# A new table of order for a two-layer hybrid encoder: where each part of a layer stands among the others, and how much a late choice of engine may bend it

## The chip, the cores and the metric

The kernel runs on one core of one Trainium2 chip, and the metric is device microseconds of one execution, measured from outside the program. The engines are named as the profile names them: PE is TensorE's matmul, PEld its weight load, DVE is VectorE, ACT is ScalarE, POOL is GpSimd, SP is SyncE, which issues the transfers. PEclk is the granted clock of TensorE as a share of 2.4 GHz; 0.50 is its lower level of 1.2 GHz. PSUM is the memory into which PE adds up its products, SBUF the one in which tiles lie.

## The reference

Two requests, a prompt of 256 tokens and a sample of 512, go through the same two layers; the kernel treats them as one block of 768 tokens with 1024 channels.

```
Layer:  h = RMSNorm(x) @ W_in, columns in four head groups
        [Fourier | differential attention | 2-D neighbourhood attention | bidirectional Mamba-2 SSD]
        x = x + concat(group outputs) @ W_out
        x = x + (silu(h2 @ w_gate) * (h2 @ w_up)) @ w_down,  h2 = RMSNorm(x)
Final RMSNorm.   D_MODEL = 1024, DEPTH = 2, D_FF = 2816, all in float32
```

The second half of a layer, SwiGLU, is called the FFN below; the first half, with its four head groups, the mixers.

## The kernel before

Float32 products are made of three matmuls in a faster format: each operand is split into a high part (a rounded copy) and a low part (operand minus high part), and low by high, high by high and high by low are added up in PSUM. Names ending in h and l are these parts. A split is therefore a copy (ACT or DVE) and a subtraction (DVE or POOL) for each tile.

**The FFN's gate and up products.** The 2816 columns are 22 blocks of 128, taken two by two as eleven pairs, `sp0` to `sp10`. The tokens are two halves of 384. With two column blocks, two halves of the input channels and two halves of the tokens, each of the matrices gate and up is a 2 by 2 block product, which is done with seven products of sums in place of eight (Strassen's way). A product is 12 matmuls of 128 by 128 by 384. `sums` makes the factors of the weights: it loads two tiles `raw` of 512 KB, splits the blocks a11 and a12, and then the sums s2, s3, s1, the block a22 and the sum s4, each into one tile `f` (its high and low part). `blocks0` and `blocks1` make the factors of the activations: b11 and b21 from token half 0 (norm `fnorm0`), and then t2, t3, t1, t4 and b22, sums over both token halves, once half 1 has its norm (`fnorm1`); `hb0` and `hb1` are the names of these parts. `first` is the products of b11 and b21, `rest` the other five, in the order t2, t3, t1, t4, b22. The results are combined on DVE (tiles u, v, c), go through Silu on ACT, and `hidden` multiplies gate by up and splits the result into ah and al.

Three pairs (`se0` to `se2`) run their `first` alone, 48 matmuls each, before `blocks1`, so that PE has work while half 1 gets its norm; their `rest` is then `sp0` to `sp2`, of 120 matmuls each. The other eight pairs have 168 each. Raw tiles of the weights have two places in SBUF (`NRAW`), so the next side's transfer can only start when the last reader of the one before is done.

**The down product** has three groups: `dn0` takes the pairs 8 to 10, whose ah and al stay in SBUF; `dn1` the pairs 0 to 3 and `dn2` the pairs 4 to 7, whose ah and al are written to DRAM (`ad`) and read back.

**What sets the order.** No engine's order is written by hand. `Schedule` takes down every operation with what it depends on, and `run` lays all of them out once, while the program is built. Each part of a layer (`self.at("sp3")` begins one) has two numbers in the table `SPAN`; an operation's key lies between them by its place in the part. Operations are sorted by key, and each engine in turn takes the first one that could start within `WAIT` of the moment at which the engine comes free. Where an operation has several ways (a copy on ACT or DVE, a subtraction on DVE or POOL), the way that ends first by the planner's costs is taken, `BIAS` being added to each engine's side:

```python
for (a, n, t), (b, *_) in zip(self.marks, self.marks[1:] + [(len(ops),)]):
    u, v = SPAN[n]
    for j in range(a, b):
        ops[j].key = t + u + (v - u) * ((j - a) / (b - a))
```

The planner also books a lock: an operation of DVE that reads two SBUF tiles, and any of POOL, is planned not to overlap the other's (`held`, `port`, `lock`). On the chip nothing of this plan's times is left, only each engine's order and the waits between engines.

Most instructions stand at lines of helpers: L402 is a matmul, L416 a transpose, L431 an activation, L435 a copy on ACT and L436 on DVE, L447 an operation with two tensors on DVE and L450 on POOL, L460 one with a scalar as well, L464 a reciprocal, L472 a reduction, L483 a transfer. In the changed kernel each is 8 lines further down.

Of the kernel before, what the change touches and what calls it, by code (L numbers as in the profile page):

```python
# [32 lines left out]
WCOLS = 1056  # L33
NSLOT, NRAW, NW, NE = 42, 2, 10, 11

WAIT = dict(PE=4, ACT=59, DVE=3, Pool=6017, Q=10)
BIAS = dict(ACT=0, DVE=300, Pool=100)
SWITCH = 255
OG = ((2, 3, 0, 1, 6, 7), (4, 5))
WPACK = 2  # L40
# [7 lines left out]
              dq0=256, dq1=384, dk0=512, dk1=640,  # L48
              nq0=1024, nq1=1152, nk0=1280, nk1=1408)
# [2 lines left out]
TABLES = {AF.Exp: 1, AF.Silu: 2, AF.Sqrt: 3}  # L52

SPAN = dict(
    fnorm0=(-8740.8, -65.3), dfin1=(-7110.3, -6348.1), dfin0=(-5181.3, -3413.1), nfin0=(-2877.4, -2819.9),
    nfin1=(-2414.8, -1862.3), fnorm1=(-1765.5, -951.1), dstk00=(-1305.8, -1205.9), dstk01=(-1140.4, -1140.4),
    sst3=(-1049.4, -990), sst5=(-947.2, -936.6), sst1=(-867, -703.1), sst6=(-864.1, -853.9), sst2=(-840.7, -648.3),
    sst4=(-740.6, -739.9), sst7=(-503.1, -498.1), sst0=(-460.4, -410.6), conv0=(-179.2, -128.4), sfin=(-99, 6.6),
    conv3=(-30.2, 11.6), fo1=(-28.8, 109.2), sch1=(-24.9, -9.3), da002=(-6, 19.9), dk1=(-5.9, -5.9),
    gate=(0.6, 16.8), norm=(2.5, 3.7), sscan=(6.4, 13.9), conv2=(17.2, 43.1), da001=(20.5, 110.7),  # L60
    da102=(20.8, 36.2), conv5=(21.2, 47.1), conv4=(42.3, 68.6), str4=(53.2, 111.3), conv1=(57.1, 57.1),
    sprep=(60.1, 72.6), dav=(66.8, 66.8), sch3=(91.5, 180.3), da100=(108.6, 115.8), sch0=(111.2, 146),
    str2=(111.6, 111.6), str0=(115.1, 134.8), str3=(123.7, 124.7), str1=(124, 124), str5=(134.7, 134.7),
    na01=(137.5, 166.3), dk0=(141.1, 183), sch5=(145.2, 148), dq0=(149.4, 149.4), sch4=(154.4, 155.1),
    sch2=(156.7, 185.3), ol=(164, 229), da012=(165.4, 215.3), fu=(175.8, 188.6), na00=(176.4, 191.1),
    da000=(183.3, 188.5), dq1=(185.2, 206.1), da004=(189.5, 201.5), fo0=(189.7, 203.4), ft=(192.8, 209.6),
    da010=(195.3, 216.1), da115=(195.6, 237.8), da005=(198.9, 200.8), da003=(202.5, 203.9), da011=(204.2, 222.9),
    fw=(208.6, 213.5), nk1=(209.2, 247.5), nav=(219.2, 245.6), da013=(220, 222), dstk10=(220.6, 220.6),
    da114=(221.9, 222.2), da105=(222.8, 231.8), da015=(223.9, 260), da103=(228.3, 228.5), da104=(229.1, 243.3),
    dstk11=(230.3, 230.3), da101=(234.6, 253.8), da014=(241.3, 248.8), nq0=(243.6, 256), da110=(245.2, 265.9),  # L70
    da113=(245.3, 246.2), na04=(246, 283.1), da112=(253.4, 253.4), nb0=(253.7, 281.3), da111=(257.5, 259.2),
    nk0=(262.3, 268), oa3=(265.2, 432.4), nq1=(269.8, 269.8), na05=(270.8, 314.2), na02=(271.6, 285),
    na03=(287.9, 327.5), na11=(291.1, 316.1), na12=(313.4, 322.2), nb1=(314.7, 349), oa4=(315.2, 342.8),
    na10=(320.3, 362.1), oa0=(328.4, 336.5), oa1=(335.9, 346.4), ow=(347.4, 373.5), oa6=(347.8, 355.8),
    na14=(369.5, 369.5), na15=(377.6, 405.7), na13=(377.9, 377.9), oa2=(385.6, 393.8), oa5=(409.1, 419.3),
    oa7=(425.8, 464.6), ob0=(449.7, 457.6), ob1=(458.4, 466.3),
    hb0=(457.5, 466), se0=(466.5, 467), se1=(467, 467.05), se2=(467.05, 467.1), hb1=(467.1, 468), xf=(467, 467.1),
    **{f"sp{p}": (470 + 28 * p, 498 + 28 * p) for p in range(11)},
    dn0=(778, 830), dn1=(830, 900), dn2=(900, 962), last=(938, 1006.8))

LAG = {("ACT", "ACT"): 153, ("DVE", "DVE"): 127, ("Pool", "Pool"): 102, ("ACT", "DVE"): 142, ("DVE", "ACT"): 140,
       ("ACT", "PE"): 281, ("DVE", "PE"): 244, ("ACT", "Pool"): 170, ("PE", "ACT"): 197, ("PE", "DVE"): 196,
# [9 lines left out]
class Schedule:  # L92
# [85 lines left out]
    def run(self):  # L178
# [32 lines left out]
        def port(o, e):  # L211
            return held["DVE" if e == "Pool" else "Pool"] if e in o.lock else 0.0
# [7 lines left out]
        def choose(e):  # L220
            f, pick = free[e], None
            for i, o in ready[e]:
# [13 lines left out]
                if len(o.ways) > 1:  # L236
                    c = next(w[1] for w in o.ways if w[0] == e) + BIAS.get(e, 0)
                    if any(max(free[w[0]], o.at[w[0]], port(o, w[0]), m) + w[1] + BIAS.get(w[0], 0) < s + c
                           for w in o.ways if w[0] != e):
                        continue  # L240
                if s <= f + WAIT[e] and (not o.table or o.table == table):
                    return s, i, o
# [1325 lines left out]
```

## Time and profile before

| | |
|---|---|
| three executions | 1857.09, 1849.77, 1855.98 us; median 1855.98 |
| profiled execution | 1856.15 us, of which the span from the first to the last instruction is 1854.4 |
| mean granted clock of TensorE | 0.986 |
| PE busy | 1771.5 us, 96% of the span |
| DVE, ACT, POOL busy | 1383.3, 794.2, 241.5 us |
| chain that ended last | PE 74%, DVE 16%, DMA 4%, ACT 3% |

The first row is the measure; the second is the one execution from which all rows of the trace come. A busy share is a mean over stages that have different limits, so the places at which PE stands idle matter, and what it waits for there.

### The profile page before, as it was taken

To read this page: it belongs to the slowest core of one execution; us is meant where nothing else is said; L and a number is where in the kernel's file an instruction comes from. 1 tells how busy PE (TensorE), PEld (TensorE's weight loads), DVE (VectorE), ACT (ScalarE), POOL (GpSimd) and SP (SyncE) were. 2 spreads that over 40 slices of the span, in tenths; PEclk is the share of its full clock that TensorE was granted. 3 is DMA by queue.
4 is the path that set the end of the run, shared out by engine and by line. 5 is a ranking of instruction groups with operands and counts; after the bars stand their busy time and mean duration, and the time that the engine had idled before them with its cause. 6 is when DMAs were issued, how large, how long until landed. Compare 5 with 4: busy or idle time off the path is not lost.

```text
span 1854.4 us, 28444 instructions
## 1 busy us (share of the span) xinstructions
PE 1771.5 (96%) x10600; PEld 1707.6 (92%) x10600; DVE 1383.3 (75%) x2646; ACT 794.2 (43%) x1660; POOL 241.5 (13%) x211
## 2 busy tenths in 40 slices
PE   8999899998899999999999988999889999999997
PEld 7998788997899999999999987889789999999987
DVE  7988897688778786434559989966978888764345
ACT  6454677463344443100234456755634344420013
POOL 0011020021131110000001211200212332110000
PEclk9999899999999999999999999999999999999999
DMA  6215446453444333642432154465343344265223
GB/s 211 91 35 157 145 145 224 146 185 103 142 136 137 113 114 119 235 162 66 113 113 74 38 162 156 136 228 176 113 142 137 116 146 137 80 229 187 92 89 114
DMA packets 96267, 252.45 MB, mean 136 GB/s; under 512 B 11648, under 2 KB 26368, under 8 KB 96128
## 3 DMA queue, kind: packets, MB, share of 16 engines
q1 hardware_dynamic: 96128, 250.62, 40.9%
q8 instruction: 84, 1.38, 0.3%
q14 instruction: 55, 0.45, 0.1%
HBM read 193.95 MB, written 56.62 MB: 135 GB/s over the span
## 4 chain that ended last, share of the span: by engine, by line
PE 74%; DVE 16%; DMA 4%; ACT 3%; issue 2%; SPq 0%; DVEq 0%; ACTq 0%
PE fm L402 34%; PE fs L402 27%; PE tok L402 6%; DMA raw<-w_up 2%; DVE f L447 1%; DVE up L447 1%; DVE nm L472 1%; DVE al L447 1%; PE ns L402 1%; DVE ex L460 1%; DVE s L447 1%; PE nv L402 1%; DMA stk<-qk 1%; DMA raw<-w_gate 1%; PE tr L416 1%
## 5 line engine op out<-in xcount | busy, mean ns | idle before, releaser
L402 PE MATMUL fm<-ah,w 128*128 128x384 f32 (+2 forms) x1408 | 268.2, 337 | 0.0
L402 PEld LDWEIGHTS fm<-ah,w 128*128 128x128 f32 x1408 | 242.9, 188 | 5.5
L402 PE MATMUL fm<-hh,w 128*128 128x384 f32 x896 | 196.0, 343 | 0.0
L447 DVE TENSOR_TENSOR w<-raw,w 128x1024 fp32r<-128x1024 f32 (+3 forms) x123 | 142.5, 1163 | 68.0 <-PE fm L402 40.3
L435 ACT ACTIVATE f<-s 128x512 fp32r<-128x512 f32 x174 | 108.4, 630 | 147.3 <-PE fs L402 81.5
L402 PEld LDWEIGHTS fm<-hh,w 128*128 128x128 f32 x896 | 158.4, 189 | 2.3
L447 DVE TENSOR_TENSOR X<-X,fm 128x384 f32<-128x384 f32 (+2 forms) x152 | 83.0, 550 | 93.8 <-PE fm L402 92.8
L402 PE MATMUL fm<-al,w 128*128 128x384 f32 (+2 forms) x704 | 142.9, 337 | 0.0
L402 PEld LDWEIGHTS fm<-al,w 128*128 128x128 f32 x704 | 123.0, 188 | 2.9
L447 DVE TENSOR_TENSOR f<-s,f 128x512 fp32r<-128x512 f32 x153 | 112.0, 739 | 16.0 <-ACT f L435 12.0
L402 PE MATMUL fm<-hl,w 128*128 128x384 f32 x448 | 113.4, 351 | 9.9 <-DVE hl L460 9.3
L402 PE MATMUL tok<-w,hh 128*128 128x256 f32 (+1 forms) x768 | 113.5, 285 | 0.0
L402 PE MATMUL fm<-oh,w 128*128 128x384 f32 x512 | 106.0, 341 | 0.0
L435 ACT ACTIVATE w<-raw 128x1024 fp32r<-128x1024 f32 (+3 forms) x70 | 67.0, 961 | 89.0 <-PE fm L402 35.6
L402 PEld LDWEIGHTS tok<-w,hh 128*128 128x128 f32 x768 | 103.7, 190 | 0.5
L435 ACT ACTIVATE f<-raw 128x512 fp32r<-128x512 f32 x108 | 67.4, 629 | 85.3 <-PE fs L402 29.9
L436 DVE CAST w<-raw 128x1024 fp32r<-128x1024 f32 (+2 forms) x64 | 43.8, 686 | 79.9 <-PE fm L402 71.3
L402 PEld LDWEIGHTS fm<-hl,w 128*128 128x128 f32 x448 | 81.1, 192 | 13.3 <-DVE hl L460 10.4
L402 PEld LDWEIGHTS fm<-oh,w 128*128 128x128 f32 x512 | 89.3, 188 | 0.8
L435 ACT ACTIVATE ah<-up 128x384 fp32r<-128x384 f32 x86 | 44.9, 523 | 94.7 <-DVE up L447 92.1
L447 DVE TENSOR_TENSOR f<-raw,f 128x512 fp32r<-128x512 f32 x109 | 82.6, 765 | 2.1 <-ACT f L435 1.3
L441 ACT ACTIVATE hh<-X,c_vec 128x384 fp32r<-128x384 f32 x31 | 17.7, 610 | 149.5 <-DVE X L447 144.0
(311 smaller groups left out, 4049.6 us busy)
## 6 DMA issues: line engine op xcount, KB each, us to landing
raw<-w_gate SPq DMA_DIRECT2D x50, 512.0 KB, 4.1
raw<-w_up SPq DMA_DIRECT2D x50, 512.0 KB, 4.0
raw<-w_down SPq DMA_DIRECT2D x40, 512.0 KB, 3.6
raw<-w_fm SPq DMA_DIRECT2D x28, 512.0 KB, 4.1
ad<-ah SPq DMA_DIRECT2D x32, 384.0 KB, 2.4
ad<-al SPq DMA_DIRECT2D x32, 384.0 KB, 2.6
ah<-ad SPq DMA_DIRECT2D x32, 384.0 KB, 7.8
al<-ad SPq DMA_DIRECT2D x32, 384.0 KB, 7.7
```

The source lines that it names most:

```text
L402: o = self.add([("PE", t, lambda: self.nc.tensor.matmul(out, lhsT, rhs, start=start, stop=stop, skip_group_check=more))], [out], [lhsT, rh ...
L416: self.add([("PE", 109, lambda: self.nc.tensor.transpose(out, in_, self.ident))], [out], [in_, self.ident], cols=2 * P)
L435: self.add([("ACT", self.acost(in_), lambda: self.nc.scalar.activation(out, in_, AF.Copy)), ("DVE", self.vcost(not self.inpsum(in_), in_), ...
L436: ("DVE", self.vcost(not self.inpsum(in_), in_), lambda: self.nc.vector.tensor_copy(out, in_))],
L441: self.add([("ACT", self.acost(in_, col), lambda: self.nc.scalar.activation(out, in_, AF.Copy, scale=col)), ("DVE", self.vcost(not self.in ...
L447: ways = [("DVE", self.vcost(False, out), lambda: self.nc.vector.tensor_tensor(out=out, in0=a, in1=b, op=op))]
L460: self.add([("DVE", self.vcost(False, a, s), lambda: self.nc.vector.scalar_tensor_tensor(out=out, in0=a, scalar=s, in1=b, op0=op0, op1=op1 ...
L472: self.add([("DVE", self.vcost(False, in_), lambda: self.nc.vector.tensor_reduce(out=out, in_=in_, axis=AX.X, op=op))], [out], [in_])
```

## The change

It changes tables alone: every number of `SPAN`, and `WAIT` and `BIAS`. The operations, what they depend on, and the places in SBUF and PSUM are the same.

```diff
-WAIT = dict(PE=4, ACT=59, DVE=3, Pool=6017, Q=10)
-BIAS = dict(ACT=0, DVE=300, Pool=100)
+WAIT = dict(PE=1.74287, ACT=18.9089, DVE=11.0577, Pool=6017, Q=10)
+BIAS = dict(ACT=-42.8228, DVE=297.384, Pool=27.3932)
...
-    **{f"sp{p}": (470 + 28 * p, 498 + 28 * p) for p in range(11)},
-    dn0=(778, 830), dn1=(830, 900), dn2=(900, 962), last=(938, 1006.8))
...
+    hb1=(497.272, 497.365), sp3=(503.623, 516.477), sp4=(515.757, 528.19), sp8=(559.987, 560.116),
```

The numbers for the pairs now stand in the order sp0, sp3, sp4, sp8, sp5, sp2, sp1, sp6, sp10, sp7, sp9; before they were sp0 to sp10. `dn0` and `dn1` lie over one another, (791.687, 880.262) and (795.438, 878.307), where dn1 began at dn0's end before. Numbered by engine, DVE has 2497 operations after 2590, and POOL 300 after 207: 202 go from DVE to POOL and 109 from POOL to DVE. In the FFN of the first layer POOL has 82 after 46, in that of the second 82 after 60. Between ACT and DVE 117 copies go each way.

**First place: DVE, at the end of `blocks1` in the first layer.** Before, `s` and `f` of pair sp0's gate (raw_1094, raw_1095) came last, among the factors t4 and b22:

```order
L447 TENSOR_TENSOR t4l_1080<-t_994_1065,t4h_1079 128x384 x2
L447 TENSOR_TENSOR t_995_1066<-t_995_1066,h_940_1011 128x384
L447 TENSOR_TENSOR s_1096<-raw_1095 128x512
L447 TENSOR_TENSOR t4l_1082<-t_995_1066,t4h_1081 128x384 x2
L447 TENSOR_TENSOR s_1097<-s_1096,raw_1094 128x512
L447 TENSOR_TENSOR b22l_1084<-y_992_1063,b22h_1083 128x384 x2
L447 TENSOR_TENSOR f_1099<-s_1097,f_1099 128x512
L447 TENSOR_TENSOR b22l_1086<-y_993_1064,b22h_1085 128x384 x2
L447 TENSOR_TENSOR s_1098<-raw_1094,raw_1095 128x512
L447 TENSOR_TENSOR f_1101<-s_1096,f_1101 128x512
```

Now they stand ahead of the first factor, t2 (t2l is its low part), and those of sp0's up side (raw_1110, raw_1111) begin there too:

```order
L455 TENSOR_TENSOR f_1100<-s_1098,f_1100 128x512
L455 TENSOR_TENSOR t_995_1066<-h_938_1009,y_993_1064 128x384
L455 TENSOR_TENSOR f_1104<-s_1103,f_1104 128x512
L455 TENSOR_TENSOR s_1112<-raw_1111 128x512
L455 TENSOR_TENSOR s_1114<-raw_1110,raw_1111 128x512
L455 TENSOR_TENSOR s_1113<-s_1112,raw_1110 128x512
L455 TENSOR_TENSOR t2l_1068<-t_994_1065,t2h_1067 128x384 x2
L455 TENSOR_TENSOR t2l_1070<-t_995_1066,t2h_1069 128x384 x2
L455 TENSOR_TENSOR up_1032<-sg_1023,fs_1028 128x384
L455 TENSOR_TENSOR up_1058<-sg_1049,fs_1054 128x384
```

All the rest of `blocks1` (t3, t1, t4, b22) has moved behind them.

**Second place: SP's queue after the first pair.** Before, the weights of sp0 (raw_1094 to raw_1111) were followed by those of sp1 (raw_1135, raw_1136), another pair of 120 matmuls:

```order
L483 DMA raw_1094<-w_gate 128x1024
L483 DMA raw_1095<-w_gate 128x1024
L483 DMA raw_1110<-w_up 128x1024
L483 DMA raw_1111<-w_up 128x1024
L483 DMA raw_1135<-w_gate 128x1024
L483 DMA raw_1136<-w_gate 128x1024
```

Now those of sp3 (raw_1217, raw_1218), a pair of 168, follow:

```order
L491 DMA raw_1094<-w_gate 128x1024
L491 DMA raw_1095<-w_gate 128x1024
L491 DMA raw_1110<-w_up 128x1024
L491 DMA raw_1111<-w_up 128x1024
L491 DMA raw_1217<-w_gate 128x1024
L491 DMA raw_1218<-w_gate 128x1024
L491 DMA ad_1126<-ah_1087 128x768
L491 DMA ad_1124<-ah_1021 128x768
L491 DMA ad_1125<-al_1022 128x768
L491 DMA ad_1127<-al_1088 128x768
L491 DMA raw_1237<-w_up 128x1024
L491 DMA raw_1238<-w_up 128x1024
```

sp2 and sp1 come sixth and seventh, between sp5 and sp6.

**Third place: POOL in pair sp8 of the first layer** (tiles made from raw_1482, raw_1483, raw_1502 and raw_1503, and al_1480). Before, POOL had two operations of the pair's sums and one low part; the rows between belong to the pairs beside it:

```order
L450 TENSOR_TENSOR s_1499<-s_1493,raw_1482 128x512
L450 TENSOR_TENSOR f_1504<-raw_1502,f_1504 128x512
L450 TENSOR_TENSOR al_1427<-up_1469,ah_1426 128x384
L450 TENSOR_TENSOR s_1548<-s_1542,raw_1531 128x512
L450 TENSOR_TENSOR f_1553<-raw_1551,f_1553 128x512
L450 TENSOR_TENSOR al_1480<-up_1522,ah_1479 128x384
```

Now it has nine:

```order
L458 TENSOR_TENSOR f_1485<-raw_1482,f_1485 128x512
L458 TENSOR_TENSOR s_1492<-raw_1483 128x512
L458 TENSOR_TENSOR f_1497<-s_1492,f_1497 128x512
L458 TENSOR_TENSOR f_1495<-s_1493,f_1495 128x512
L458 TENSOR_TENSOR f_1496<-s_1494,f_1496 128x512
L458 TENSOR_TENSOR f_1517<-s_1512,f_1517 128x512
L458 TENSOR_TENSOR f_1518<-raw_1503,f_1518 128x512
L458 TENSOR_TENSOR f_1325<-raw_1323,f_1325 128x512
L458 TENSOR_TENSOR s_1335<-raw_1323,raw_1324 128x512
L458 TENSOR_TENSOR f_1338<-s_1333,f_1338 128x512
L458 TENSOR_TENSOR al_1480<-up_1523,ah_1479 128x384
L458 TENSOR_TENSOR al_1480<-up_1522,ah_1479 128x384
```

The seven f and s of sp8 stand in one run, and the next pair's (raw_1323) follow at once.

## Rows read from the trace of the kernel before

**Rows 1.** Page, part 1: busy time of each engine

```profile
PE 1771.5 (96%) x10600; PEld 1707.6 (92%) x10600; DVE 1383.3 (75%) x2646; ACT 794.2 (43%) x1660; POOL 241.5 (13%) x211
```

**Rows 2.** Windows: length, busy time (instructions) by engine, clock, DMA

```profile
417.60:464.00 46.40, 38.18 (x203) 36.60 (x201) 39.66 (x70) 18.19 (x35) 7.87 (x5) 0.93 0.31 107
464.00:510.40 46.40, 40.70 (x212) 39.81 (x213) 35.85 (x60) 17.20 (x31) 7.65 (x5) 0.93 0.41 143
...
1484.80:1531.20 46.40, 46.40 (x266) 46.05 (x265) 38.77 (x61) 20.70 (x38) 15.35 (x10) 1.00 0.44 146
```

**Rows 3.** PE's waits in 375 to 575: total us, times, longest

```profile
PE fs L402 <- ACT f L435: 12.8, 4, 6.4
```

**Rows 4.** PE's waits in 1290 to 1470

```profile
PE fs L402 <- ACT f L435: 12.2, 4, 6.4
```

**Rows 5.** Timeline of PE: start, us, operation, idle time before it

```profile
428.97 0.69 PE L402 MATMUL fs<-t1l,f 128*128 128x384 f32 x1 [6.37 <-ACT f L435]
...
467.46 1.01 PE L402 MATMUL fs<-t1l,f 128*128 128x384 f32 x2 [3.96 <-ACT f L435]
...
492.54 0.79 PE L402 MATMUL fs<-t1l,f 128*128 128x384 f32 x3 [1.97 <-ACT f L435]
...
1342.37 1.01 PE L402 MATMUL fs<-t1l,f 128*128 128x384 f32 x2 [6.42 <-ACT f L435]
```

**Rows 6.** Windows of PE behind these waits: busy, clock

```profile
428.97:433.79 4.82, 4.82 (x17) 0.60 0.00 0
433.79:438.65 4.86, 4.86 (x29) 1.00 0.66 208
467.46:471.20 3.74, 3.73 (x14) 0.61 0.00 0
492.54:497.67 5.13, 5.13 (x19) 0.67 0.25 57
1342.37:1347.50 5.13, 5.13 (x16) 0.50 0.00 0
```

**Rows 7.** Timeline of DVE and ACT from the norm to the first sum

```profile
401.58 0.55 DVE L472 TENSOR_REDUCE rt<-nrm 128x3 f32<-128x384 f32 x1
...
427.34 0.68 DVE L447 TENSOR_TENSOR s<-raw 128x512 f32<-128x512 f32 x1
...
428.31 0.61 ACT L435 ACTIVATE f<-s 128x512 fp32r<-128x512 f32 x1
```

**Rows 8.** Chain of waits of 458 to 468: start, us, what

```profile
459.59 6.38 DMA raw<-w_up
...
466.08 0.63 ACT f L435
```

**Rows 9.** Window of one full pair (columns as rows 2)

```profile
578.00:606.60 28.60, 28.60 (x164) 28.31 (x163) 23.05 (x38) 11.45 (x21) 4.00 (x3) 1.00 0.39 129
```

**Rows 10.** Groups by form on POOL: busy us, mean ns

```profile
L450 POOL TENSOR_TENSOR f<-s,f 128x512 fp32r<-128x512 f32 x23 | 35.4, 1547 | 89.0 <-ACT f L435 89.0
```

**Rows 11.** Timeline: POOL beside DVE in a pair

```profile
454.28 1.60 POOL L450 TENSOR_TENSOR f<-raw,f 128x512 fp32r<-128x512 f32 x1
454.66 1.78 DVE L447 TENSOR_TENSOR f<-s,f 128x512 fp32r<-128x512 f32 x1
```

**Rows 12.** Timeline: last reload of ah and al ahead of dn0, and dn0's first matmul

```profile
743.64 0.32 SPq L483 DMA_DIRECT2D al<-ad  x1
...
744.62 0.86 PE L402 MATMUL fm<-al,w 128*128 128x384 f32 x4
```

**Rows 13.** Window at the reloads (columns as rows 2)

```profile
740.00:745.00 5.00, 5.00 (x31) 5.00 (x30) 3.46 (x6) 1.90 (x3) 0.13 (x1) 1.00 1.03 414
```

**Rows 14.** PE's longest waits in the first layer's mixers, 100 to 375

```profile
PE sc L402 <- DMA stk<-qk: 2.5, 1, 2.5
PE tr L416 <- DVE ex L460: 2.4, 2, 1.4
PE pq L402 <- ACT ex L431: 1.7, 1, 1.7
```

More of the change, by code (lines that the diff above doesn't have):

```diff
@@ L54 @@
 SPAN = dict(
[L55 to L74, printed above, removed]
@@ L75 @@
-    na14=(369.5, 369.5), na15=(377.6, 405.7), na13=(377.9, 377.9), oa2=(385.6, 393.8), oa5=(409.1, 419.3),
-    oa7=(425.8, 464.6), ob0=(449.7, 457.6), ob1=(458.4, 466.3),
-    hb0=(457.5, 466), se0=(466.5, 467), se1=(467, 467.05), se2=(467.05, 467.1), hb1=(467.1, 468), xf=(467, 467.1),
-    **{f"sp{p}": (470 + 28 * p, 498 + 28 * p) for p in range(11)},
-    dn0=(778, 830), dn1=(830, 900), dn2=(900, 962), last=(938, 1006.8))
+    dfin0=(-15625.014, -366.538), da114=(-7079.262, -7074.19), fo0=(-7068.535, -6858.243),
@@ new lines @@
+    da115=(-7063.099, -6831.567), sst7=(-7014.889, -6855.18), da105=(-6797.763, -6774.465),
+    sst2=(-6458.275, -6213.333), da000=(-6455.256, -6054.611), sch1=(-6197.979, -6184.396),
+    sst0=(-6135.573, -5938.665), dfin1=(-5223.138, -4663.299), fnorm1=(-5218.269, -3900.298),
+    fnorm0=(-6554.734, -1580.954), nfin1=(-2696.185, -1723.14), ol=(-1688.544, -1522.028),
+    dstk00=(-1089.481, -1017.001), da002=(-1111.924, -613.172), sst5=(-765.114, -726.599),
+    dstk01=(-717.267, -717.267), sst1=(-1272.838, 250.82), sprep=(-231.506, -52.254), da001=(-310.19, 53.178),
@@ new lines @@
+    conv2=(-44.476, -3.438), conv0=(-58.446, 41.319), norm=(5.34, 9.841), gate=(27.352, 44.961), dk1=(26.967, 48.278),
+    conv1=(44.813, 44.813), conv5=(47.121, 47.121), str1=(-11.457, 108.975), conv4=(47.651, 66.462),
+    conv3=(45.805, 77.41), sst4=(0.471, 142.7), sfin=(92.178, 92.178), str4=(64.064, 121.95), sscan=(89.446, 99.766),
+    sst3=(86.849, 102.49), dav=(97.313, 105.075), sst6=(107.52, 131.062), da102=(22.393, 216.493),
+    str5=(128.145, 128.145), str0=(123.662, 132.918), sch0=(110.207, 147.683), str3=(120.123, 144.179),
@@ new lines @@
+    sch3=(85.92, 185.168), sch2=(93.374, 186.479), str2=(144.402, 145.442), sch5=(143.107, 147.334),
+    fo1=(54.93, 248.09), dq0=(152.158, 152.817), da100=(154.444, 163.592), dk0=(140.824, 185.62),
+    sch4=(158.579, 168.944), na00=(104.603, 243.96), fu=(184.731, 185.595), da012=(169.012, 214.455),
+    dq1=(185.41, 206.156), da004=(194.275, 202.864), da005=(196.995, 202.682), ft=(191.016, 211.506),
+    da003=(202.808, 202.808), nfin0=(154.684, 252.115), da010=(195.777, 213.271), da011=(203.062, 219.086),
@@ new lines @@
+    fw=(208.034, 217.028), xf=(194.804, 238.77), dstk10=(219.419, 220.431), da013=(220.035, 220.05),
+    nav=(214.547, 240.942), nk1=(210.224, 247.598), na01=(145.948, 315.602), dstk11=(231.516, 231.516),
+    da104=(228.88, 237.28), da103=(223.959, 246.023), da112=(236.854, 237.612), da015=(223.797, 260.261),
+    da101=(235.3, 253.973), da014=(241.524, 248.915), da113=(245.125, 247.665), nq0=(244.174, 256.656),
+    da110=(244.999, 264.72), da111=(256.81, 258.395), nk0=(263.626, 264.157), oa4=(267.41, 271.151),
@@ new lines @@
+    na04=(268.259, 272.844), nb0=(257.906, 284.907), nq1=(271.646, 276.133), na05=(276.221, 281.754),
+    na02=(297.438, 297.438), na03=(272.735, 374.366), oa0=(322.412, 325.958), na12=(302.396, 351.31),
+    nb1=(319.609, 339.804), oa6=(327.048, 332.845), oa1=(304.57, 364.098), oa3=(260.84, 430.812),
+    oa2=(364.211, 364.211), na11=(364.775, 367.645), na15=(368.764, 368.764), na14=(373.767, 376.815),
+    na10=(375.828, 376.429), na13=(339.597, 419.212), oa7=(381.482, 384.567), ow=(430.016, 430.679),
@@ new lines @@
+    oa5=(439.403, 439.403), ob0=(443.747, 443.747), ob1=(458.899, 459.36), se0=(453.174, 466.05),
+    hb0=(462.525, 470.3), se2=(468.725, 468.725), se1=(469.31, 472.49), sp0=(477.524, 508.167),
+    hb1=(497.272, 497.365), sp3=(503.623, 516.477), sp4=(515.757, 528.19), sp8=(559.987, 560.116),
+    sp5=(562.067, 562.067), sp2=(562.727, 592.739), sp1=(597.816, 610.077), sp6=(625.881, 625.881),
+    sp10=(627.253, 629.358), sp7=(644.578, 682.229), sp9=(691.263, 764.317), dn0=(791.687, 880.262),
+    dn1=(795.438, 878.307), dn2=(917.252, 937.425), last=(1221.069, 1268.032))
```

## The prediction

> **What bounds the kernel now.** The page's first part comes first: PE is busy for 1771.5 us, 96% of the span, and no other engine is near that [rows 1]. So PE's work stays, and what an order can win is PE's idle time (span less busy, 83 us) and time at the lower clock. The windows come second. In most slices of the FFN PE is full, as in 1484.8 to 1531.2; the holes stand at the FFN's start, 417.6 to 510.4 in the first layer, where PE is busy for 38.2 and 40.7 us of 46.4 at a clock of 0.93 [rows 2]. Third, the waits by cause: around the FFN's start PE waits in each layer for `f`, the high part of a weight sum, 12.8 and 12.2 us, 6.4 of them at one place [rows 3, 4]. The timeline says where: before the first t product (t1, 6.37 and 6.42 us), and then in the pairs sp1 and sp2 (3.96, 1.97) [rows 5]. Behind each, PE runs slowly. From 428.97 its clock is 0.60 and 17 matmuls take 4.82 us; the next 29 take 4.86 us at 1.00, 0.168 each [rows 6]. At that pace the 17 would have taken 2.86, so 1.96 us were lost; 14 in 3.74 and 19 in 5.13 lose 1.39 and 1.94. That is 5.3 us in the first layer, and as much taken for the second, whose first stretch is worse (16 in 5.13 at 0.50, a loss of 2.4) [rows 6]. So 25.0 us of waits and about 10.7 of slow clock, some 36 us, hang on the start of the two FFNs. The mixers' waits are many and small, the longest 2.5 us [rows 14].
>
> **The first t product.** From the norm's reduction (401.58) to the sum s for t1's weight (427.34) DVE works through 50 instructions in 25.8 us, 0.52 each; ACT's f follows at 428.31 and PE goes on at 428.97 [rows 5, 7]. PE had 105 matmuls between the norm's last transpose and this product, in the order of its rows, and ran dry. Before, sp0's sums stood behind nearly all factors; now they stand ahead of t2, which is also the product that comes first. Counted in the order, DVE has 38 instructions up to the last t2l, 38 by 0.54 (0.52 and a little for POOL's part of them) or 20.5 us, and PE has 118 matmuls to cover it, 118 by 0.17 and the transposes' lag of 0.9, or 21 us. So this wait goes to about nothing. What is late next is the rest of `blocks1`: 31 DVE instructions (16.7 us) stand between t2l and b22l, and PE has 84 matmuls (14.3 us) meanwhile: 2.4 us of new wait. I take 2.5 us a layer in place of 6.4: 12.8 becomes 5.0, **−7.8**. Bounds: all of it (−12.8), or 5 us left in each layer (−3).
>
> **sp1 and sp2.** With two raw places, the up side's transfers start only when the gate side's last sum is made: the chain shows the transfer for 6.38 us from 459.59, then ACT's f at 466.08, and PE waits 3.96 us for it [rows 5, 8]. A side of a 120-matmul pair is 60 matmuls, 10.1 us, too little for sums, transfer and split; a side of a 168 pair is 14.1 us. Now sp0 is followed by sp3, whose two `first` products need only a11 and a12, split straight from the raw tile, and sp2 and sp1 come after four long pairs. In the order the first use of sp3's up side stands 49 matmuls behind the issue of its transfer, 8.2 us against some 7 of transfer and split. The waits left over in rows 3 and 4 are 6.4 and 5.8 us; I leave 1.0 a layer: **−10.2**. Bounds −12.2, and −5 if sp2 and sp1 stall as before for want of a raw place.
>
> **The slow clock.** It came behind holes of 2 to 6 us [rows 5, 6]. With 7 us of holes left of 25, and these in smaller pieces, I take a third of the 10.7 as staying: **−7.0**, bounds 0 and −10.7.
>
> **More work on POOL.** An f takes POOL 1547 ns [rows 10]. DVE's stretch in a full pair is 38 instructions in 23.05 us, 0.61 each [rows 9]. A move saves DVE 0.6 and costs POOL 1.5, and the two don't run freely side by side: a DVE f that began 0.38 us into a POOL operation took 1.78 us and ended with it or soon after [rows 11]. Were they never to run together, sp8 would need 32 by 0.61 on DVE and 9 by 1.5 on POOL, 33.0 us against PE's 28.6; sp5 with seven, 31.2 against 28.6; sp2 (33 operations, nine on POOL) 28.1 against 120 by 0.17 or 20.4; sp1 with six, 25.5 against 20.4. But in 1484.8 to 1531.2 DVE was busy for 38.77 us and POOL for 15.35, together 54.1 in 46.4, and PE was never idle: at least half of POOL's time lay beside DVE's [rows 2]. With half of it so, sp8 needs 26.3, sp5 25.9, sp2 21.4 and sp1 21.0: only sp2 and sp1 stand over, by 1.6 us a layer. I take 2 a layer: **+4**. Bounds 0 (no gain, since PE did not wait in such pairs before), and the four excesses in full, 4.4 + 2.6 + 7.7 + 5.1 or 20 a layer.
>
> The Trainium skill speaks against this part of the change ("SBUF — State Buffer", section "Who interferes with whom"): a VectorE instruction with two SBUF inputs and a GpSimd instruction that reads SBUF shut each other out for a whole instruction, while one with at most one SBUF input goes on. The trace agrees on the pair in rows 11, and by that rule alone the sum would lie at its upper bound; the 54.1 us in rows 2 say that enough of DVE's work is of the other kind.
>
> **dn0 over dn1.** Before, the last reload ahead of dn0's first matmul was issued 1 us before it, behind some 14 others, and the transfers ran at 414 GB/s, the DMA engines full [rows 12, 13]. Now 16 reloads of dn1 stand in SP's queue ahead of most of dn0's residual X, while w_down for both groups alternates. By positions in the order, the first dn1 matmul that reads the last al comes about 4 us after that tile can have landed at the rate of rows 13, and dn0's reads of the last pair's al come within 1 us of when it was made before. Taken +0.5 a layer, **+1**; bounds 0 (PE did not wait there before) and +8 a layer (half of 16 tiles by 384 KB at 414 GB/s, 15 us, unhidden).
>
> **Mixers and end.** All their parts are moved. Some covers between maker and reader grow in the order (the first softmax transposes 44 to 53 matmuls) and some shrink (ab of the Fourier part 35 to 12, yo of the Mamba part 90 to 9). With waits of some 15 us a layer in pieces like rows 14, I take **0**, bounds −8 and +8 over both. At the end one output comes some 50 matmuls sooner: **−0.5**. The start of the kernel is unchanged.
>
> Sum: −7.8 − 10.2 − 7.0 + 4 + 1 − 0.5 = −20.5, against the profiled 1856.15: 1835.7; that execution stands 0.2 over the median of the three. **I predict 1836 us.**
>
> **Rivals.** (1) *The waits only move.* DVE has 16.7 us of factors against PE's 14.3 behind the first product, and sp2 and sp1 stay short pairs. If the 2.4 becomes 5, sp2 and sp1 keep half of their waits (6) and the clock is lost as before, what stays is −3 − 6 + 4 or −5: **1851**, no change. For it: DVE is busy for 39.7 of 46.4 us there [rows 2]. Against: less than before stands ahead of each wait. (2) *POOL shuts DVE out.* If DVE's instructions that read PSUM queue behind one that is locked out, nothing overlaps, and the four pairs sp8, sp5, sp2 and sp1 cost 20 a layer where I have 2: 1836 + 36 = **1872**, slower. It decides where DVE and POOL together pass PE's time in the pair, 28.6 or 20.4 us. For it: POOL's nine in sp8 come in a run. Against: rows 2. (3) *dn1's reloads are late*, 8 a layer: **1851**. (4) *More is won*: the waits and the slow clock vanish wholly, and the mixers give half of their bound: −25.0 − 10.7 − 4 + 4 + 1 − 0.5, **1821**.
>
> **Chances.** The forecast, 1826 to 1846, 0.55; (1) 0.16; (2) 0.09; (3) 0.08; (4) 0.12. A measurement of this kernel tells about 0.5%, 9.3 us, from no change. Faster than 1846.7: the forecast and (4) but 0.02, and 0.06 of (1) and (3) together, 0.71. Slower than 1865.3: (2) and 0.01, 0.10. The rest, 0.19, within 0.5%. The range leaves out (2) and the lowest end of (4): 1814 to 1858.
>
> **What would show it.** Right: PE's waits for f in the first 80 us after the norm under 8 us over both layers, the first product t2 with a wait under 3, no window of the FFN's start under a clock of 0.96, PE full in sp3, sp4 and sp8. Wrong: PE waits for f of over 2 us in sp8, sp2 or sp1 with POOL just ended (rival 2); waits for t3l, t4l or b22l of 5 us (rival 1); fm waiting for a transfer into ah or al (rival 3); the mixers' waits changed by over 8 us, which I could not price.

## The result and the profile after

| | before | changed |
|---|---|---|
| median of four executions | 1855.15 us (1849.77 to 1857.09) | 1827.92 us (1824.90 to 1829.14) |
| ratio, 95% interval | | 0.9855 [0.9831, 0.9880] |
| span of the profiled execution | 1854.4 | 1826.4 |
| mean granted clock | 0.986 | 0.997 |

Faster by 27 us where 20 were forecast. The page's first part of the changed kernel answers to [rows 1]: PE is busy for 8 us less with the same matmuls, DVE for 11 less, POOL for 135 more.

```profile
PE 1763.1 (97%) x10600; PEld 1695.2 (93%) x10600; DVE 1372.4 (75%) x2553; ACT 801.8 (44%) x1664; POOL 376.7 (21%) x304
```

The windows of the changed kernel at the FFN's start, and one in the second layer's pairs, in the columns of [rows 2]:

```profile
417.60:464.00 46.40, 43.59 (x239) 40.78 (x238) 41.84 (x67) 19.17 (x39) 12.99 (x10) 1.00 0.23 80
464.00:510.40 46.40, 46.40 (x266) 46.28 (x266) 38.82 (x60) 18.23 (x34) 17.41 (x12) 1.00 0.36 127
1299.20:1345.60 46.40, 44.22 (x245) 41.99 (x244) 44.56 (x78) 25.04 (x51) 17.96 (x8) 1.00 0.19 58
1484.80:1531.20 46.40, 45.78 (x261) 45.04 (x260) 37.27 (x55) 19.27 (x35) 17.68 (x14) 1.00 0.48 159
```

The first two were at 38.18 and 40.70 with a clock of 0.93 [rows 2]; now they have 43.59 and 46.40 at 1.00. The last one was full, and has lost 0.6 us. PE's waits in the changed kernel in 375 to 575, the stretch of [rows 3]:

```profile
PE fs L410 <- DVE t3l L455: 1.8, 3, 1.2
PE fs L410 <- ACT u L443: 1.1, 1, 1.1
PE fs L410 <- ACT f L443: 0.6, 2, 0.5
```

The waits for f, 12.8 us before, are 0.6. To compare whole kernels, the 1848 matmuls of a layer's gate and up products (tile fs) can be cut out whole, since nearly no other product stands among them in any kernel. By the first and the last start of such a matmul, the kernels fall into five stretches of us:

| | to the first fs | fs, layer 0 | to the next fs | fs, layer 1 | to the end | span |
|---|---|---|---|---|---|---|
| before | 394.5 | 350.0 | 563.3 | 349.9 | 196.7 | 1854.4 |
| changed | 392.1 | 336.3 | 562.3 | 337.0 | 198.7 | 1826.4 |
| e_first | 393.2 | 344.7 | 566.0 | 347.4 | 196.7 | 1848.0 |
| e_pairs | 393.1 | 341.0 | 564.8 | 342.8 | 196.8 | 1838.5 |
| e_both | 391.9 | 340.6 | 561.5 | 343.7 | 196.7 | 1834.4 |
| e_ffn | 393.2 | 337.2 | 565.8 | 338.9 | 197.2 | 1832.3 |
| e_mixers | 405.3 | 345.3 | 562.4 | 345.0 | 196.7 | 1854.7 |
| e_wb | 408.3 | 341.9 | 582.8 | 341.5 | 199.6 | 1874.1 |
| e_unpairs | 404.4 | 336.8 | 562.3 | 343.2 | 199.6 | 1846.3 |
| e_nopool | 396.3 | 330.0 | 568.6 | 329.9 | 197.3 | 1822.1 |
| e_load10 | 406.2 | 344.0 | 563.5 | 334.7 | 198.0 | 1846.4 |
| e_old_dve | 391.4 | 347.7 | 563.5 | 344.5 | 196.6 | 1843.7 |
| e_ffn_dve | 390.2 | 329.0 | 563.0 | 331.7 | 198.5 | 1812.4 |
| e_best | 391.0 | 330.9 | 561.9 | 329.8 | 196.3 | 1809.9 |

Each row is one execution. Four executions of the kernel before lie 7.3 us apart, so 2 or 3 us in one stretch are at the edge of what such a row can show.

Of the change's 28.0 us of span, 13.7 and 12.9 lie in the two fs stretches, 3.4 in the stretches with the mixers, and the end has lost 2.0. The windows over the two fs stretches (0.4 us longer, for the last matmul), first of the kernel before:

```profile
394.50:744.90 350.40, 334.53 (x1857) 327.73 (x1856) 282.13 (x468) 147.59 (x270) 61.64 (x43) 0.98 0.38 126
1307.80:1658.10 350.30, 334.11 (x1858) 328.25 (x1857) 285.20 (x454) 147.18 (x270) 85.11 (x57) 0.98 0.38 127
```

then of the changed one:

```profile
392.10:728.80 336.70, 330.08 (x1857) 322.57 (x1857) 279.31 (x428) 142.29 (x264) 119.62 (x79) 1.00 0.40 134
1290.70:1628.10 337.40, 330.41 (x1858) 322.32 (x1856) 278.42 (x426) 141.22 (x264) 118.55 (x76) 1.00 0.40 135
```

PE's idle time, length less busy, went from 15.9 and 16.2 to 6.6 and 7.0 us: 18.5 us. Its busy time went down by 4.5 and 3.7, 8.2 us, with the clock from 0.98 to 1.00.

### The profile page after: what moved, and what is told of

Read it like the earlier page. It is cut to its first block, busy times and chain, and to the rows that moved or that the text cites. A ratio compares the mean times of both kernels' runs of the same rounds, so it can differ in the third digit from the quotient of the medians.

```text
span 1826.4 us, 28370 instructions
## 1 busy us (share of the span) xinstructions
PE 1763.1 (97%) x10600; PEld 1695.2 (93%) x10600; DVE 1372.4 (75%) x2553; ACT 801.8 (44%) x1664; POOL 376.7 (21%) x304
## 4 chain that ended last, share of the span: by engine, by line
PE 58%; DVE 23%; DMA 7%; ACT 7%; issue 4%; SPq 0%; POOL 0%; DVEq 0%; ACTq 0%; POOLq 0%
PE fm L410 31%; PE fs L410 16%; PE tok L410 4%; DMA raw<-w_up 4%; DVE f L455 4%; ACT f L443 2%; DMA raw<-w_gate 2%; DVE nm L480 2%; DVE s L455 1%; DVE up L455 1%; PE ns L410 1%; DVE al L455 1%; PE nv L410 1%; ACT ex L439 1%; DVE at L455 1%
## 5 line engine op out<-in xcount | busy, mean ns | idle before, releaser
L410 PE MATMUL fm<-ah,w 128*128 128x384 f32 (+2 forms) x1408 | 283.8, 337 | 0.0
L443 ACT ACTIVATE w<-raw 128x1024 fp32r<-128x1024 f32 (+3 forms) x76 | 74.6, 983 | 258.9 <-PE fm L410 195.9
L410 PE MATMUL fm<-al,w 128*128 128x384 f32 (+2 forms) x704 | 160.7, 337 | 1.2 <-DMA al<-ad 1.2
L455 DVE TENSOR_TENSOR f<-s,f 128x512 fp32r<-128x512 f32 x124 | 107.0, 873 | 20.8 <-ACT f L443 20.0
L410 PE MATMUL tok<-w,hh 128*128 128x256 f32 (+1 forms) x768 | 119.6, 285 | 0.0
L458 POOL TENSOR_TENSOR f<-s,f 128x512 fp32r<-128x512 f32 x52 | 81.6, 1581 | 139.2 <-ACT f L443 139.2
L443 ACT ACTIVATE f<-raw 128x512 fp32r<-128x512 f32 x100 | 62.4, 629 | 98.7 <-DMA raw<-w_up 46.7
L444 DVE CAST w<-raw 128x1024 fp32r<-128x1024 f32 (+3 forms) x58 | 39.1, 674 | 54.3 <-PE fm L410 43.0
```

Source lines behind the costliest of these rows:

```text
L410: o = self.add([("PE", t, lambda: self.nc.tensor.matmul(out, lhsT, rhs, start=start, stop=stop, skip_group_check=more))], [out], [lhsT, rh ...
L443: self.add([("ACT", self.acost(in_), lambda: self.nc.scalar.activation(out, in_, AF.Copy)), ("DVE", self.vcost(not self.inpsum(in_), in_), ...
L444: ("DVE", self.vcost(not self.inpsum(in_), in_), lambda: self.nc.vector.tensor_copy(out, in_))],
L455: ways = [("DVE", self.vcost(False, out), lambda: self.nc.vector.tensor_tensor(out=out, in0=a, in1=b, op=op))]
L458: lambda: self.nc.gpsimd.tensor_tensor(out=out, in0=a, in1=b, op=op)))
```

## The experiments

**e_first: the numbers at the FFN's start alone.**

```diff
-    hb0=(457.5, 466), se0=(466.5, 467), se1=(467, 467.05), se2=(467.05, 467.1), hb1=(467.1, 468), ...
+    hb0=(462.525, 470.3), se0=(453.174, 466.05), se1=(469.31, 472.49), se2=(468.725, 468.725),
+    hb1=(497.272, 497.365), sp0=(477.524, 497.9), ...
```

> The kernel before with seven numbers of the new table alone: hb0, hb1, se0 to se2 and sp0 (its end kept at 497.9, so that sp1 follows). sp0's sums then stand ahead of the factor t2, and sp1 and sp2 still follow sp0. If the first t product's wait is a matter of DVE's order there (my step), PE's wait of 6.4 us a layer falls to 1 to 3 and the slow clock behind it goes: -7.8 - 4 = about -12 us, ratio 0.993 to 0.995, with the waits at sp1 and sp2 (4.0, 2.0) left. If the wait only moves (rival), the next product waits instead and the ratio is 0.998 to 1.000.

1849.93 against 1855.71 us, ratio 0.9962 [0.9948, 0.9975]: 6 to 7 us, half of what was expected. The timeline of PE shows the first product, now t2, still waiting, and behind it sp1:

```profile
427.47 2.23 PE L403 MATMUL fs<-t2l,f 128*128 128x384 f32 x5 [4.78 <-DVE t2l L448]
...
485.69 1.24 PE L403 MATMUL fs<-t1l,f 128*128 128x384 f32 x3 [2.60 <-ACT f L436]
```

The wait shrank from 6.4 to 4.8 and stands at another factor. e_both, below, shows the reason.

**e_pairs: the order of the pairs alone.**

```diff
-    **{f"sp{p}": (470 + 28 * p, 498 + 28 * p) for p in range(11)},
+    **{f"sp{p}": (470 + 28 * i, 498 + 28 * i) for i, p in enumerate((0, 3, 4, 8, 5, 2, 1, 6, 10, 7, 9))},
```

> The kernel before with the eleven pairs in the new order (sp0, 3, 4, 8, 5, 2, 1, 6, 10, 7, 9) on the old spacing of 28, nothing else. If short pairs behind short pairs cause the waits at sp1 and sp2, they go, 10 us of waits and 6 us of slow clock: about -16 us, ratio 0.991, while the first t product still waits 6.4 us a layer. If a short pair stalls wherever it stands (rival 1), sp2 and sp1 wait 2 to 4 us each in their new places and the ratio is 0.997 to 1.000.

1838.45 us, ratio 0.9907 [0.9893, 0.9922]: 17 us, as expected, the largest single piece. No wait for f is left in either layer but the one before the first t product, which has grown:

```profile
431.01 1.01 PE L402 MATMUL fs<-t1l,f 128*128 128x384 f32 x2 [8.19 <-ACT f L435]
```

**e_both: the two together, all else as before.**

> The kernel before with two pieces of the new table together: the seven numbers at the FFN's start (hb0, hb1, se0 to se2, sp0) and the new order of the pairs; old mixers, WAIT, BIAS, dn. Alone they gave -7 and -17 us. If they are two separate waits, they add: about -24 us, ratio 0.987, and what the rest of the change gives is some 3 us. If the second takes part of what the first takes (both move sums ahead on DVE and ACT), the ratio is 0.990 to 0.992.

1835.52 against 1857.67 us, ratio 0.9878 [0.9863, 0.9892]: 22 us, and 6 plus 17 would be 23. They add, and the two pieces give most of the change's 27 us. The t2l wait of 4.8 us is there in both layers. DVE's timeline, from the norm's reduction:

```profile
400.44 0.54 DVE L473 TENSOR_REDUCE rt<-nrm 128x3 f32<-128x384 f32 x1
...
419.91 0.55 DVE L448 TENSOR_TENSOR t2l<-t,t2h 128x384 fp32r<-128x384 f32 x1
420.38 0.69 DVE L448 TENSOR_TENSOR s<-raw 128x512 f32<-128x512 f32 x1
...
427.75 1.01 DVE L448 TENSOR_TENSOR t2l<-t,t2h 128x384 fp32r<-128x384 f32 x2
428.69 0.68 DVE L448 TENSOR_TENSOR f<-s,f 128x512 fp32r<-128x512 f32 x1
429.29 0.54 DVE L448 TENSOR_TENSOR t2l<-t,t2h 128x384 fp32r<-128x384 f32 x1
```

The four t2l are not in one piece: the sums of sp0's up side stand among them, so that the last one is DVE's 48th instruction and begins after 29 us. The reduction also stands 8.5 us behind the first fs, in the changed kernel 3.7. These few numbers, under the old WAIT and BIAS, do not make the order that I had counted.

**e_ffn and e_mixers: the old table's numbers put back for one half of the layer,** in the changed kernel, with the new WAIT and BIAS.

> The changed kernel with the old numbers for the parts of the mixers; the FFN's numbers, WAIT and BIAS are new. If the gain is the FFN's (my sum, mixers 0), the ratio to before is that of the changed kernel, 0.984 to 0.988. If the mixers' new order gave a share (their slow clock at 181 to 232 is gone after the change), it is 0.989 to 0.992.

1835.31 us, ratio 0.9892 [0.9875, 0.9909]. The fs stretches are within 1 and 2 us of the changed kernel's, those ahead of them 1.1 and 3.5 us longer. That is the second expectation: beside the FFN's new numbers, the mixers' are worth some 6 us.

> The changed kernel with the old numbers for the FFN (norms, hb, se, sp, dn0, dn1); only the mixers' parts, dn2, the end, WAIT and BIAS are new. If the mixers gave nothing: 0.998 to 1.002, with the waits for f at the FFN's start as before. If they gave a share through the clock: 0.994 to 0.997, and no slow clock before the FFN.

1855.12 us, ratio 0.9990 [0.9978, 1.0002]: nothing on the whole, but not nothing anywhere. The fs stretches are 5 us shorter each, and the way to the first one is 11 us longer. The two kernels' gains, 20 us and none, don't add up to the change's 27. Both have the new WAIT and BIAS; these two with the whole old table were not run, so what they do by themselves is not known.

**e_wb: SPAN new, WAIT and BIAS old.**

```diff
-WAIT = dict(PE=1.74287, ACT=18.9089, DVE=11.0577, Pool=6017, Q=10)
-BIAS = dict(ACT=-42.8228, DVE=297.384, Pool=27.3932)
+WAIT = dict(PE=4, ACT=59, DVE=3, Pool=6017, Q=10)
+BIAS = dict(ACT=0, DVE=300, Pool=100)
```

> The changed kernel with the old WAIT and BIAS; only SPAN is new. POOL then has 265 operations where the changed kernel has 300 and the kernel before 207. If SPAN makes the gain and WAIT and BIAS only shift work between engines: 0.984 to 0.988. If the share of POOL in the new BIAS costs 2 us a layer or more, it is faster than the changed kernel by 2 to 5 us; if the new BIAS and WAIT win something in the mixers, slower by as much.

1879.00 us, ratio 1.0111 [1.0087, 1.0135], slower than before, which none of the expectations had. The fs stretches gain 8 us each against before, and the stretches with the mixers lose 14 and 20. The window of the mixers in this kernel has PE at a clock of 0.95:

```profile
92.80:408.00 315.20, 291.44 (x1879) 270.98 (x1878) 256.92 (x618) 184.37 (x448) 47.72 (x38) 0.95 0.43 139
```

In the changed kernel it is 1.00, and the fs begin 16 us sooner:

```profile
92.80:400.00 307.20, 291.93 (x1930) 271.63 (x1928) 265.45 (x622) 190.06 (x461) 60.20 (x50) 1.00 0.47 149
```

So the new SPAN gains only with the new WAIT and BIAS, of the two settings that were run. Which of WAIT and BIAS it needs, and at which operation, stays open.

**e_unpairs: the pairs' order undone in the changed kernel,** sp0 to sp10 on the new slots.

> The changed kernel with the eleven pairs put back in the order sp0 to sp10 on the new table's slots, nothing else. If the order of the pairs is worth 16 to 17 us here too: 1844 us, ratio 0.993 to 0.996, with waits for f of 3 to 4 us at sp1 and sp2 and slow clock behind them. If the new BIAS and WAIT cover the short pairs as well (rival), 0.986 to 0.989.

1847.99 us, ratio 0.9945 [0.9928, 0.9962]. The waits for f are back where they were:

```profile
468.83 1.65 PE L411 MATMUL fs<-t1l,f 128*128 128x384 f32 x4 [2.93 <-ACT f L444]
...
1367.34 0.62 PE L411 MATMUL fs<-t1l,f 128*128 128x384 f32 x2 [2.79 <-ACT f L444]
...
1394.03 1.01 PE L411 MATMUL fs<-t1l,f 128*128 128x384 f32 x2 [3.04 <-ACT f L444]
```

But the fs stretches lose only 0.5 and 6.2 us. Most of the 20 us is the first layer's mixers, 12.3 us longer though no number of theirs was touched: in 278.4 to 324.8 alone PE is idle for 6.7 us at a clock of 0.93, where the changed kernel has 0.1 us and 1.00. The total would have been taken for the price of the pairs' order, and it is not.

**e_nopool: POOL's BIAS at 3000 in the changed kernel.**

> The changed kernel with POOL's BIAS at 3000, so that all but a few small operations of POOL go to DVE; POOL is idle. If POOL's work costs through the shared port (my +4), this is 2 to 6 us faster than the changed kernel, 1822 to 1826. If POOL's help to DVE is needed at the FFN's start and in the short pairs (33 operations by 0.61 are 20.1 us against 20.4), PE waits for DVE there and it is 5 to 15 us slower, 1833 to 1843.

1824.03 us, ratio 0.9819 [0.9802, 0.9837], 4 us under the changed kernel's median: the total is what my +4 asked for, by two larger parts of opposite sign. The fs stretches fall by 6.3 and 7.1 us, those with the mixers grow by 4.2 and 6.3. The first fs window of this kernel:

```profile
396.30:726.70 330.40, 327.37 (x1857) 323.09 (x1857) 272.00 (x496) 147.15 (x271) 0.16 (x3) 1.00 0.41 138
```

DVE does 496 operations in 272.0 us here; in the changed kernel, with 68 fewer, it is busy for 279.3. POOL's 119.6 us relieve DVE of nothing.

**e_ffn_dve and e_old_dve: POOL left out of the FFN alone,** from its first norm to its last pair, in the changed kernel and in the one before.

```diff
-        if pool and not self.inpsum(out, a, b):
+        if pool and not self.inpsum(out, a, b) and not self.dve:
...
+        self.dve = True
         self.blocks0(L)
...
+        self.dve = False
         for g, fs in enumerate(FGROUPS):
```

> The changed kernel with POOL left out of the FFN alone (from its first norm to its last pair); in the mixers and the norms POOL keeps its work. With POOL idle everywhere the 1848 gate and up matmuls of a layer took 330 us where the changed kernel takes 336 to 337, and the mixers 4 to 6 us more. If POOL's work costs in the FFN and pays in the mixers, this is 12 to 13 us faster than the changed kernel, about 1815, ratio 0.977 to 0.980. If the gain in the FFN was the luck of another order, 1822 to 1830.

1814.95 against 1857.26 us, ratio 0.9768 [0.9752, 0.9785], 13 us under the changed kernel's median. The fs stretches are those of e_nopool, the mixers those of the changed kernel.

> The kernel before with POOL left out of the FFN alone. There POOL was busy for 62 and 85 us in the two FFNs. If each us of POOL there costs 0.05 to 0.06 us, as 119 us cost 6.5 in the changed kernel, the FFNs lose 3.5 and 4.5: ratio 0.995 to 0.997. If the waits at the FFN's start hide it or POOL was needed in blocks1, 0.999 to 1.004.

1847.89 us, ratio 0.9946 [0.9931, 0.9961], a little more than expected: 2.3 and 5.4 us in the fs stretches, 3 in the first mixers. The second fs window of this kernel, with POOL idle:

```profile
1302.60:1647.50 344.90, 330.62 (x1857) 327.16 (x1856) 279.19 (x505) 151.75 (x274) 0.00 (x0) 0.98 0.38 128
```

DVE is busy for 279.2 where it was 285.2, with 51 instructions more.

**e_load10: more work for POOL, of use to nobody.**

```diff
         n = 4 * P
+        z = self.lamv[:, :P]
+        for i in range(10):
+            self.add([("Pool", 148 + 2.1 * P, lambda: self.nc.gpsimd.tensor_tensor(out=z, in0=z, in1=self.ones, op=ALU.mult))],
+                     [z], [z, self.ones], lock=("DVE", "Pool"))
         raw = []
```

> The changed kernel with ten more operations on POOL for each side of a pair, 128 wide, which multiply a constant that nobody reads any more by ones: 560 more in all, some 0.4 us each, 235 us of POOL's time in the FFNs, booked by the planner like the others. POOL is then busy for some 33 of 46.4 us in the pairs and DVE for 38. If POOL shuts out all of DVE while it reads SBUF (rival 2), 71 us of work stand in 46.4 and the kernel is over 200 us slower. If DVE's operations that read PSUM and half of the rest go on beside it (my step), the pairs need 54 and it is some 50 to 100 slower. If nearly all of it lies beside DVE's work, under 10.

1850.28 us, ratio 0.9959 [0.9944, 0.9973], 22 us over the changed kernel. Since these operations wait for nothing, more than half of the 560 ran in the first layer's mixers, which are 14 us longer, and none in the second fs stretch. In the first one POOL has 165 operations more than in the changed kernel:

```profile
406.20:750.60 344.40, 331.98 (x1858) 324.16 (x1857) 294.64 (x430) 145.75 (x267) 204.71 (x244) 1.00 0.38 130
```

With 85 us more of POOL the stretch is 7.7 us longer. The load did not come evenly to the pairs, as all three expectations had it, and none of their sizes fits. It still tells something of rival 2. The two busy times, 499 us in 344, don't: an operation that waits for the other engine counts as busy. But take 0.55 us for each of DVE's 430 operations, e_nopool's mean, and for each of POOL's the shortest that one of its shape took in any run (0.40 us for those added). That is 236 and 146 us, an estimate, and one behind the other they would need 382. So not everything runs one at a time.

**e_best: e_ffn_dve with dn1 behind dn0,** dn0=(778, 835), dn1=(835.1, 900).

> The same as e_ffn_dve, and dn1 behind dn0 instead of over it: dn0=(778, 835), dn1=(835.1, 900). If dn0 over dn1 costs the 0.5 us a layer that I put down, or nothing, this equals e_ffn_dve within 1 us. If the reloads of dn1 were late in the changed kernel (rival 3), it gains up to 8 us a layer behind the last gate and up matmul.

1811.76 us, ratio 0.9753 [0.9738, 0.9767], the best of all, and 3 us under e_ffn_dve, run beside it. The end is 2.2 us shorter. In the changed kernel PE waited there for a reload:

```profile
1748.04 2.13 PE L410 MATMUL fm<-al,w 128*128 128x512 f32 x8 [1.19 <-DMA al<-ad]
```

This wait is not in e_best. The last ten reloads are issued from 1737.7 to 1742.2 in the changed kernel, and from 1661.3 to 1667.3 in e_best.

## Why the prediction was right, and where its sizes were off

**The bound.** PE's work stayed, and the gain is its idle time at the FFN's start and the clock behind it, as the waits and windows before had said. The signs named for it came: PE waits for f for 0.6 us a layer, does not wait at the first product t2, and the windows there are at 1.00.

**The first t product and the short pairs.** Forecast −7.8 and −10.2, together −18.0; PE's idle time in the fs stretches fell by 18.5. In the changed kernel DVE comes from the norm's reduction at 395.75 to the last t2l at 417.3, 21.5 us where I had 20.5, and PE does not wait there. What is late next is not b22l, as I had put it, but t3l, 1.8 us in place of my 2.5. The operand x of t3 was given to POOL:

```profile
408.58 9.57 POOL L458 TENSOR_TENSOR x<-y,x 128x384 f32<-128x384 f32 x1 [18.53 <-DVE h L455]
```

Where DVE makes x (e_nopool, e_ffn_dve), the wait for t3l is 0.6 us.

Under the old numbers the pairs' order alone gives 17 us (16 expected for that run, waits and clock), the start's numbers alone 6 (12 expected): the short pairs were the larger part. Undone in the changed kernel (e_unpairs), the order costs the fs stretches only 0.5 and 6.2 us, though PE waits there for f for 5.6 and 6.9 us: no wait for t3l is left, and POOL is busy for 22 and 27 us less. The step that I counted from DVE's rows holds for the order in which I counted, 38 instructions in the changed kernel, and not for 48 in e_both.

**The slow clock.** Forecast −7.0, a third staying; PE's busy time in the fs stretches fell by 8.2, and their windows show 1.00. This term was mis-sized, since the slow clock went wholly: no hole of over 1.31 us is left there. The 8.2 is not the clock alone. PE's busy time also holds short waits between matmuls: e_nopool, at the same 1.00, has 327.4 us in the first layer where the changed kernel has 330.1. The first layer's mixers, at 0.89 in 185.6 to 232 before, are at 1.00 too, but their stretch gained only 2.4 us.

**POOL.** Forecast +4 for both layers, as an excess in sp2 and sp1, from half of POOL's time lying beside DVE's. That the size fits is luck: the place and the reading behind it were wrong. In the changed kernel PE is full in sp2, and idle in sp1 for 0.4 us a layer; with POOL out of the FFN (e_ffn_dve) the two pairs are shorter by 0.6 and 0.7 us a layer. What is shorter then is above all sp0, by 2.8 us in each layer, sp7 by 2.1 and 1.8, and sp3 by 1.1 and 1.2; sp8 is longer by 0.7 and 1.1. These are sp2 and sp0 of the changed kernel's first layer and sp0 of e_ffn_dve, cut at the pairs' first matmuls:

```profile
564.80:585.80 21.00, 21.00 (x122) 20.98 (x121) 17.10 (x26) 8.33 (x15) 10.22 (x10) 1.00 0.48 175
...
420.00:444.80 24.80, 22.62 (x123) 20.73 (x122) 22.98 (x39) 8.13 (x17) 6.17 (x5) 1.00 0.14 44
...
418.00:439.90 21.90, 21.33 (x121) 20.79 (x120) 21.12 (x44) 8.28 (x17) 0.00 (x0) 1.00 0.15 49
```

In sp0 DVE is busy for longer with fewer operations, and PE's wait for t3l, above, falls into it. In all, the changed kernel's fs stretches are 7.3 and 5.3 us shorter without POOL, 7.1 of these 12.6 us as idle time of PE. Those of the kernel before are 2.3 and 5.4 shorter (e_old_dve). That is a net figure, since PE waits longer for the first f there, 7.57 us where it was 6.37 [rows 5]:

```profile
428.35 1.01 PE L402 MATMUL fs<-t1l,f 128*128 128x384 f32 x2 [7.57 <-ACT f L435]
```

So in the kernel before POOL helped at that place and cost elsewhere. By these single executions its net cost is 12.6 us now and was 7.7; the change added about 5, to a cost that I had not seen.

The reading that failed is that of [rows 2]. DVE's 38.77 and POOL's 15.35 us in 46.4 I took for work side by side; but a DVE operation that waits for POOL counts as busy. The f of [rows 11] took 1.78 us, and an f<-s,f takes 0.69 with POOL idle. With 0.55 us for each of DVE's 61 operations, e_nopool's mean, the two are 48.9 us, an estimate: some 2.5 us lay side by side, and not 7.7. The slowing on which rival 2 rests is there, at 12.6 us in all where it had 40; that nothing overlaps is not (e_load10).

**dn0 over dn1, mixers, end.** Forecast +1, 0 and −0.5; measured −3.4 in the two stretches with the mixers, the second of which also holds the first layer's down product, and +2.0 at the end. The end is rival 3 in small: a reload of ah and al that is 1.2 us late, in the last group and not in the place where I had looked.

The sum: −18.5 − 8.2 − 3.4 + 2.0 = −28.1, against −20.5. The gap of 7.6 is the clock (1.2), the mixers (3.4), the +1 for dn0 over dn1, which does not show, and 4.5 in PE's idle time, where I had −18.0 with POOL's +4 and 18.5 went; the end takes 2.5 of it back. The 4.5 come from waits that I had left out of the count of 25 us for f. PE's idle time in the fs stretches was 32.1 us: waits for u were another 4.2, those for f's low part on DVE 1.7.

## What to carry to other kernels

A list of engine times doesn't tell whether a second engine helps: compare the first engine's busy time with and without it. Here 68 operations moved from DVE to POOL left DVE as busy as before, and the work that was to relieve it cost 6 us a layer. Where a planner lays out the whole program, a change in one place can move others (12 us in mixers of which no number was changed), so cut the trace at landmarks that every kernel has and compare stretch by stretch, not totals.

## What the runs showed of the hardware that was not expected

**POOL slows DVE operations with two SBUF inputs, and not those that read PSUM.** The same groups of DVE in the first FFN of three kernels, 390 to 760 us, by form (busy us, mean ns): f<-s,f reads two SBUF tiles, u<-u,fs one and PSUM. With POOL idle (e_nopool):

```profile
L456 DVE TENSOR_TENSOR f<-s,f 128x512 fp32r<-128x512 f32 x88 | 59.6, 686 | 15.4 <-ACT f L444 14.4
L456 DVE TENSOR_TENSOR u<-u,fs 128x384 f32<-128x384 f32 x44 | 24.1, 547 | 2.3 <-PE fs L411 2.1
L445 DVE CAST f<-raw 128x512 fp32r<-128x512 f32 x11 | 4.7, 423 | 4.7 <-DMA raw<-w_gate 2.9 <-DMA raw<-w_up 1.7
```

Before, with 62 us of POOL in the stretch:

```profile
L447 DVE TENSOR_TENSOR f<-s,f 128x512 fp32r<-128x512 f32 x82 | 59.5, 731 | 6.8 <-ACT f L435 4.1
L447 DVE TENSOR_TENSOR u<-u,fs 128x384 f32<-128x384 f32 x44 | 24.1, 548 | 12.1 <-PE fs L402 12.0
```

Changed, with 120:

```profile
L455 DVE TENSOR_TENSOR f<-s,f 128x512 fp32r<-128x512 f32 x62 | 53.6, 873 | 10.3 <-ACT f L443 9.9
L455 DVE TENSOR_TENSOR u<-u,fs 128x384 f32<-128x384 f32 x44 | 24.1, 547 | 10.0 <-PE fs L410 9.8
L444 DVE CAST f<-raw 128x512 fp32r<-128x512 f32 x15 | 7.9, 524 | 6.7 <-DMA raw<-w_up 5.0 <-DMA raw<-w_gate 1.5
```

The one goes from 686 over 731 to 873 ns, the other stays at 547. The Trainium skill has this rule ("SBUF — State Buffer", section "Who interferes with whom"): an instruction of VectorE with two SBUF inputs contends with one of GpSimd that reads SBUF, and one with at most one SBUF input, outside VectorE's two-port modes, does not. The trace agrees with it for these two groups. The copies f<-raw, with one SBUF input, are slower too, 423 and 524 ns in the rows above, but take 426 in e_load10; what makes the difference stays open. Nor does the slowing go by POOL's busy time alone: in e_load10, with 205 us of POOL in the fs stretch, mostly short operations, f<-s,f took 829 ns.

**The loser can be POOL, and for long.** The x above stood on POOL for 9.57 us from 408.58, where the five operations of its size that followed in the next 13 us took 1.0 to 1.6. In that time DVE ran operations with two SBUF inputs one behind the other, without a gap, and its first one that reads PSUM, and so only one SBUF tile, is the up in this row of its timeline:

```profile
417.20 1.00 DVE L455 TENSOR_TENSOR up<-sg,fs 128x384 f32<-128x384 f32 x2
```

POOL ended 0.95 us later. In the second layer the same pair of x took 11.11 us together, as in the first. The planner costs such an operation at 0.95 us. In e_first it is another operation of POOL, t, and the first up on DVE comes sooner:

```profile
409.54 6.02 POOL L451 TENSOR_TENSOR t<-h,y 128x384 f32<-128x384 f32 x1 [8.34 <-DVE h L448]
...
414.60 1.01 DVE L448 TENSOR_TENSOR up<-sg,fs 128x384 f32<-128x384 f32 x2
```

Here too DVE has no gap, and POOL ends 0.96 us after the up begins. So a dense run of such operations on DVE held POOL off, and in both kernels it ended about 0.95 us after DVE's first operation that reads PSUM began. A run that ends in a gap instead was not tried.
